# Half of the other two column blocks of a down projection by seven block products, and its operand sums made by accumulating transfers

## The chip, the cores and the metric

The kernel runs on one core of a Trainium2 chip. The metric is device time in microseconds (us), the median of three runs. A profile is one further execution of the same program, recorded by the hardware profiler.

## The reference

Two layers of an encoder on 256 tokens of 2048 numbers in float32. Each layer has an attention part, which this change doesn't touch, and an MLP (multi-layer perceptron) with 8192 inner columns:

```python
    h = rmsnorm(x, norm_mlp[l])
    u = jax.nn.relu(jnp.einsum('bsd,df->bsf', h, w_up[l]))
    x = x + jnp.einsum('bsf,fd->bsd', u * u, w_down[l])
```

The last line is the down projection: 256 x 8192 by 8192 x 2048.

## The kernel before

**Precision.** TensorE (PE) multiplies in a rounded 32-bit format. So each operand is split into a rounded part ("hi") and its remainder ("lo"), and a product of two operands is made of three: hi by hi, lo by hi, hi by lo. Weights arrive from memory in tiles of 128 x 1024 (512 KB). `split` (L1013, L1014) makes the two parts: ScalarE (ACT) casts to `whi`, then VectorE (DVE) subtracts into `wlo`. There are three buffers for each of the two.

**Steps.** The program is a list of steps, one for each weight tile or sum of tiles. The main loop goes through the list. At step i it issues on the SyncE (SP) queue the loads up to step i+6, emits the splits up to step i+2, and emits the preparations (`prep`) up to step i+4 (`LOOK_PREP` = 5), and then the products of step i. What it emits is put by the tile framework into one fixed instruction order for each engine, and each engine works its list strictly in that order.

**Groups.** The 8192 inner columns are worked in 8 groups of 1024. For each group there are 16 up steps (`up_steps`, L673 and L678: eight products of 512 columns and eight of 256, from which ACT and DVE make `uT` and, in `sums_of`, `sT`), and the down steps of the same group of rows of `w_down`, for four blocks of 512 output columns, j = 0 to 3. Up steps of group g+1 are mixed with down steps of group g.

**Plain down steps** (`down_steps`, helper `mode_b`, L466) take one tile of 256 rows of one block j: 12 products of 128 x 512 (two blocks of tokens, two blocks of rows, three parts). In groups 0 to 5 the blocks j = 2 and 3 take four such steps each. Their sum stays in two PSUM banks and is added to the residual `x` by DVE at the end (L723).

**Seven products** (`strassen_steps`, L795). The blocks j = 0 and 1 are worked as a product of 2 x 2 blocks: two blocks of tokens, rows of `w_down` in an even and an odd half, two blocks of columns. Seven products (P1, P2, P7, P6, P5, P3, P4 in this order) take the place of eight, at the price of sums on both sides. The sums of the left side are `sT`. On the right, with B11, B12, B21, B22 the four tiles as stored, P1 uses B11 and P2 uses B21; then B11 gets B12 added (call it B11'), P7 uses B12 + B22, P6 uses t2 = B22 + B11', P5 uses B11', P3 uses B22, and P4 uses t2 + B21. Every product is made for two tiles (h = 0, 1), so there are 14 steps of 6 products of 128 x 512. After the second tile the bank is added to or taken from `x` by DVE (L771). Three banks are in use: "b" from the common pool of six, and "a" and "d", the two halves of the tile `S`, of which there is one.

**The sums on the right** are made in two ways. B11' and t2 + B21 come by an accumulating transfer: a DMA issued on the GpSimd (POOL) queue (`on_top`, L781) that adds the tile from memory to what lies in the buffer. B12 + B22 (L816) and t2 (L822) are additions of 128 x 1024 on DVE.

The tiles B12 and B22 lie in the pool `side` (four buffers, loads at L993), B11 in `spare0` or `spare1` (one buffer each), t2 in the pool `big` (24 buffers).

## Time and profile before

| | |
|---|---|
| median of 3 runs | 2006.74 us (2006.64 to 2006.88) |
| the profiled execution's own time | 2007.62 us |
| its span, first to last instruction | 2005.8 us |
| mean granted TensorE clock | 0.999 |
| PE busy | 1992.2 us, 10206 products |
| DVE, ACT, POOL busy | 1600.0, 1216.0, 337.8 us |
| memory traffic | 420.62 MB, 210 GB/s over the span |
| groups 0 to 5 of the first layer | about 365 to 875 us of the span |

Groups of instructions are named by the line, the engine, the operation and the buffers (output, then inputs); behind the bar stand their busy time, the mean time of one, and the idle time of the engine before them with what ended it. The windows give the busy time of each engine in a stretch. "PEld" is the loading of the left operand into the array, which runs beside the products. In the chain of waits each piece has its start, its length and its line.

### The profile page before, as it was taken

The page shows a single profiled execution, that of the slowest core. Times are in us where ns is not written, and L with a number is a line of the kernel's source. Part 1 is how long each engine was busy: PE and PEld are TensorE (multiplying, and loading weights), DVE is VectorE, ACT ScalarE, POOL GpSimd, SP SyncE. Part 2 cuts the span into 40 slices and gives each one's busy share as a digit, 9 for nine tenths or more (in the row PEclk, how much of TensorE's full clock was granted, in tenths as well). Part 3 has the DMA queues.
Part 4 walks back from the last instruction along what each step waited for, and adds up shares of the span by engine and source line. Part 5 has one row for each costly group of instructions (what it writes and reads, how often), then busy time and mean ns, then how long its engine had stood idle before and what let it go on. Part 6 is the DMA issues. An engine that isn't in the chain of part 4 may idle for free.

```text
span 2005.8 us, 28051 instructions
## 1 busy us (share of the span) xinstructions
PE 1992.2 (99%) x10206; PEld 1698.6 (85%) x10206; DVE 1600.0 (80%) x2121; ACT 1216.0 (61%) x1742; POOL 337.8 (17%) x394
## 2 busy tenths in 40 slices
PE   9999999999999999999999999999999999999998
PEld 7888888888888888888888888888888888888887
DVE  6777877878788888888857688777888888888887
ACT  7657756565655656566657677565655556565664
POOL 0674520000000000000008745100000000000000
PEclk9999999999999999999999999999999999999999
DMA  9755655778787787877766465557787776877774
GB/s 338 215 160 158 210 167 190 218 211 239 210 234 212 218 224 207 246 207 235 207 190 197 147 179 196 179 190 215 208 245 215 232 211 208 243 210 237 198 236 144
DMA packets 118838, 420.62 MB, mean 210 GB/s; under 512 B 13571, under 2 KB 15875, under 8 KB 118700
## 3 DMA queue, kind: packets, MB, share of 16 engines
q1 hardware_dynamic: 109052, 384.18, 59.3%
q0 software_dynamic: 9216, 33.56, 10.2%
q8 instruction: 80, 1.31, 0.3%
q10 hardware_dynamic: 432, 1.10, 0.1%
q14 instruction: 58, 0.48, 0.1%
HBM read 412.99 MB, written 2.11 MB: 207 GB/s over the span
## 4 chain that ended last, share of the span: by engine, by line
PE 95%; DVE 1%; DMA 1%; ACT 1%; issue 1%; SPq 0%; POOL 0%; POOLq 0%; DVEq 0%; ACTq 0%
PE mm L466 40%; PE mm L673 23%; PE S L795 13%; PE mm L678 12%; PE mm L795 2%; PE tr L380 1%; DMA wraw<-in_w_in_dram 1%; PE tr L399 1%; PE S L343 1%; PE S L342 1%; PE tr L223 1%; DVE wlo L1014 0%; ACT big L360 0%; PE tr L392 0%; PE tr L255 0%
## 5 line engine op out<-in xcount | busy, mean ns | idle before, releaser
L1014 DVE TENSOR_TENSOR wlo<-wraw,whi 128x1024 fp32r<-128x1024 f32 (+1 forms) x553 | 680.3, 1232 | 241.5 <-ACT whi L1013 238.7
L1013 ACT CAST whi<-wraw 128x1024 fp32r<-128x1024 f32 (+1 forms) x553 | 579.9, 1051 | 453.8 <-PE mm L466 170.8
L466 PE MATMUL mm<-whi,big 128*128 128x512 f32 (+1 forms) x2172 | 613.2, 386 | 0.6 <-ACT whi L1013 0.6
L673 PE MATMUL mm<-big,whi 128*128 128x512 f32 x2048 | 509.5, 391 | 0.0
L466 PEld LDWEIGHTS mm<-whi,big 128*128 128x128 f32 x2172 | 404.4, 188 | 80.2 <-ACT whi L1013 1.6
L673 PEld LDWEIGHTS mm<-big,whi 128*128 128x128 f32 x2048 | 377.6, 188 | 74.5
L466 PE MATMUL mm<-wlo,big 128*128 128x512 f32 (+1 forms) x1086 | 355.5, 384 | 0.0
L678 PEld LDWEIGHTS mm<-big,wlo 128*128 128x128 f32 x2048 | 279.4, 190 | 20.0
L678 PE MATMUL mm<-big,wlo 128*128 128x256 f32 x2048 | 285.6, 282 | 0.0
L466 PEld LDWEIGHTS mm<-wlo,big 128*128 128x128 f32 x1086 | 204.3, 188 | 38.0
L795 PE MATMUL S<-whi,big 128*128 128x512 f32 x768 | 209.1, 394 | 0.0
L781 POOL DMA_DIRECT2D spare<-in_w_down_dram x32 | 28.0, 876 | 745.8 <-DVE wlo L1014 671.2
L795 PEld LDWEIGHTS S<-whi,big 128*128 128x128 f32 x768 | 134.9, 189 | 21.3 <-DVE x L771 1.0
L466 PE MATMUL mm<-spare,big 128*128 128x512 f32 (+1 forms) x606 | 140.2, 380 | 0.0
L466 PEld LDWEIGHTS mm<-spare,big 128*128 128x128 f32 x606 | 108.9, 188 | 20.4
L795 PE MATMUL S<-wlo,big 128*128 128x512 f32 x384 | 118.8, 391 | 0.0
L781 POOL DMA_DIRECT2D big<-in_w_down_dram x32 | 27.7, 866 | 492.4 <-DVE wlo L1014 485.5
L1013 ACT CAST whi<-big 128x1024 fp32r<-128x1024 f32 x64 | 67.2, 1050 | 70.3 <-PE mm L673 50.4
L1013 ACT CAST whi<-side 128x1024 fp32r<-128x1024 f32 x64 | 67.2, 1051 | 65.4 <-PE mm L673 41.2
L1014 DVE TENSOR_TENSOR wlo<-big,whi 128x1024 fp32r<-128x1024 f32 x64 | 78.3, 1224 | 32.7 <-ACT whi L1013 32.6
L1013 ACT CAST whi<-spare 128x1024 fp32r<-128x1024 f32 x64 | 67.4, 1053 | 52.1 <-PE mm L673 40.8
L1014 DVE TENSOR_TENSOR wlo<-spare,whi 128x1024 fp32r<-128x1024 f32 x64 | 78.0, 1219 | 23.9 <-ACT whi L1013 23.8
(158 smaller groups left out, 2100.3 us busy)
## 6 DMA issues: line engine op xcount, KB each, us to landing
wraw<-in_w_up_dram SPq DMA_DIRECT2D x256, 512.0 KB, 4.4
wraw<-in_w_down_dram SPq DMA_DIRECT2D x160, 512.0 KB, 4.1
wraw<-in_w_in_dram SPq DMA_DIRECT2D x119, 512.0 KB, 3.7
wraw<-in_w_o_dram SPq DMA_DIRECT2D x64, 512.0 KB, 3.7
side<-in_w_down_dram SPq DMA_DIRECT2D x64, 512.0 KB, 4.4
spare<-in_w_down_dram SPq DMA_DIRECT2D x32, 512.0 KB, 4.5
spare<-in_w_down_dram POOLq DMA_DIRECT2D x32, 512.0 KB, 5.8
big<-in_w_down_dram POOLq DMA_DIRECT2D x32, 512.0 KB, 6.5
```

What stands on the lines that cost most here:

```text
L223: nc.tensor.transpose(psv[:, kk, t, :], x[:, t, c0:c0 + P], ident)
L342: nc.tensor.matmul(o, st, u.kh[:, kh, :], start=True, stop=False)
L343: nc.tensor.matmul(o, st, u.kl[:, kh, :], start=False, stop=True)
L380: nc.tensor.transpose(ps[:, c * P:(c + 1) * P], u.p[:, s, kb * P:(kb + 1) * P], ident)
L399: nc.tensor.matmul(ps, u.V[:, kb, u.kv, :, :], pt[:, kb, :], start=n == 0, stop=n == 3)
L466: nc.tensor.matmul(banks[t][:, 0:n], a, (wl if part == "hl" else wh)[:, i, :], start=first and i == 0 and part == "hh", stop=last and i == ...
L673: nc.tensor.matmul(box["b"][fs], wh[:, kk, fs * P:(fs + 1) * P], ht, start=s == 0 and kk == 0, stop=False, skip_group_check=True)
L678: nc.tensor.matmul(box["b"][fs][:, 0:256], wl[:, kk, fs * P:(fs + 1) * P], ht[:, 0:256], start=False, stop=s == 3 and kk == 3, skip_group_ ...
L781: nc.gpsimd.dma_start(tile, src(par, j, h).rearrange("p (k n) -> p k n", k=2), accum_op=ALU.add)
L795: nc.tensor.matmul(o, ops[i][a], w[:, i, :], skip_group_check=True, start=fresh and h == 0 and i == 0 and a == 0 and w is wh, stop=h == 1 ...
L1013: last_act[0] = nc.scalar.copy(h[:, part], w[:, part]).ins
L1014: last_lo[0] = nc.vector.tensor_sub(lo[:, part], w[:, part], f(h[:, part])).ins
```

## The change

In groups 0 to 5 of both layers the blocks j = 2 and 3 are also worked by seven products, for one of the two tiles only (`strassen_steps(g, 1, (0,), 4)`: 7 steps of 6 products). The other half of the rows stays with plain steps: two of 12 products for j = 3 (`down_steps((g,), 3, (2, 3))`), and two for j = 2 at the end of the group, which go on summing into the banks "b" and "d" of the second set of seven products. So the second set isn't evacuated after P2 and P4, and these two plain steps evacuate both.

In all groups B12 + B22 is now made by an accumulating transfer as well, prepared up to seven steps ahead of its use (`LOOK_T3`). Of the sums on the right only t2 is left on DVE. In the first set it is prepared up to six steps ahead (`LOOK_T2` = 7), in the second set up to three (4).

The order of steps within groups 0 to 5 is new: one step of seven products, alternating with an up or plain step, two of the first set being neighbours in two places; then the second set alternating with seven up steps; and at the end the two plain steps of j = 2. The next group begins at once with its first P1. Numbering the 41 steps of a group from 0, the first set stands at 0, 2, 4, 6, 8, 10, 12, 14, 15, 17, 19, 21, 22, 24, the second at 26, 28, ... 38, the plain steps of j = 2 at 39 and 40. Before, a group had 38 steps and began with two plain steps. `w_down` is packed differently on the host, so that each tile is still one contiguous block. The argument `skip_group_check` concerns a check at build time.

```diff
-    LOOK_LOAD, LOOK_SPLIT, LOOK_PREP, BUDGET = 7, 2, 5, 2.2
+    LOOK_LOAD, LOOK_SPLIT, LOOK_PREP, LOOK_T2, LOOK_T3, BUDGET = 7, 2, 5, 7, 8, 2.2
...
-        def down_steps(gs, j):
+        def down_steps(gs, j, ks=range(4), shared=None):
             out_, box = [], {}
-            tiles = [(g, k) for g in gs for k in range(4)]
+            tiles = [(g, k) for g in gs for k in ks]
...
-                        box["b"] = [mm_bank(), mm_bank()]
+                        box["b"] = [shared["b"], shared["d"]] if shared else [mm_bank(), mm_bank()]
...
-                    mode_b(box["b"], hts, wh, wl, [0, 1], n == 0, last, blocks=(0,) if final else (0, 1),
+                    mode_b(box["b"], hts, wh, wl, [0, 1], n == 0 and not shared, last, blocks=(0,) if final else (0, 1),
...
-                out_.append(Step(w_down[l, (g * 4 + j) * 4 + k], 2, 512, None, mm, fourth=gs == (7,)))
+                ti = (g * 4 + j) * 4 + k if g >= 6 else g * 16 + 12 + (j - 2) * 2 + k - 2
+                out_.append(Step(w_down[l, ti], 2, 512, None, mm, fourth=gs == (7,)))
             return out_
-        def strassen_steps(g):
+        def strassen_steps(g, pair=0, tiles=(0, 1), look=LOOK_T2):
...
             raw, t2, box, done = {}, {}, {}, set()
             def src(par, j, h):
-                return w_down[l, g * 16 + (par * 2 + j) * 2 + h]
+                return w_down[l, g * 16 + ((par * 2 + j) * 2 + h if pair == 0 else 8 + par * 2 + j)]
...
+            def sum_of(to, a, b):
+                with tc.issue_after(last_lo[0]):
+                    nc.vector.tensor_add(to, a, b)
             def on_top(tile, par, j, h):
                 nc.gpsimd.dma_start(tile, src(par, j, h).rearrange("p (k n) -> p k n", k=2), accum_op=ALU.add)
             out_ = []
             for name, lf, bk, fresh, dst in plan:
-                for h in range(2):
+                for h in tiles:
                     def mm(wh, wl, name=name, lf=lf, bk=bk, fresh=fresh, dst=dst, h=h):
                         if (name, h) == ("P1", 0):
...
-                                                 stop=h == 1 and i == 1 and w is wl)
-                        if h == 1:
+                                                 stop=h == tiles[-1] and i == 1 and w is wl)
+                        if h == tiles[-1] and not (pair and name in ("P2", "P4")):
                             evac(o, *dst)
                             if g == 7 and name in ("P3", "P4"):
                                 layer_end(l, dst[1])
                     loads, prep, get = [], None, None
                     if name == "P1":
-                        loads = [(("B11", h), src(0, 0, h), lambda h=h: spare(F32, h))]
+                        loads = [(("B11", h), src(0, 0, h), lambda h=h + pair: spare(F32, h))]
                         get = lambda h=h: raw["B11", h]
                     elif name == "P2":
+                        loads = [(("B12", h), src(0, 1, h), None)]
                         def prep(h=h):
                             assert ("P1", h) in done
                             on_top(raw["B11", h], 0, 1, h)
                     elif name == "P7":
-                        loads = [(("B12", h), src(0, 1, h), None), (("B22", h), src(1, 1, h), None)]
                         def prep(h=h):
-                            with tc.issue_after(last_lo[0]):
-                                nc.vector.tensor_add(raw["B12", h], raw["B12", h], raw["B22", h])
+                            on_top(raw["B12", h], 1, 1, h)
                         get = lambda h=h: raw["B12", h]
                     elif name == "P6":
+                        loads = [(("B22", h), src(1, 1, h), None)]
                         def prep(h=h):
                             t2[h] = big(F32, 2, 512)
-                            with tc.issue_after(last_lo[0]):
-                                nc.vector.tensor_add(t2[h], raw["B22", h], raw["B11", h])
+                            sum_of(t2[h], raw["B22", h], raw["B11", h])
                         get = lambda h=h: t2[h]
                     elif name == "P5":
                         def prep(h=h):
...
                         done.add(key)
                         return get()
                     stp = Step(src(1, 0, h) if name == "P2" else None, 2, 512, None, mm, fourth=False, prep=prep,
+                               look={"P6": look, "P7": LOOK_T3}.get(name, LOOK_PREP),
                                raw=operand if get else None,
                                loads=[(raw, k, v, w) for k, v, w in loads])
                     out_.append(stp)
-            return out_
+            return out_, box
         steps.extend(up_steps(0))
         for g in range(8):
             if g < 6:
-                ss = down_steps((g,), 2) + down_steps((g,), 3) + up_steps(g + 1)
+                up = up_steps(g + 1)
+                ss = up[0:4] + down_steps((g,), 3, (2, 3)) + up[4:]
             elif g == 6:
                 ss = up_steps(7)
             else:
                 ss = down_steps((6, 7), 2) + down_steps((6,), 3) + down_steps((7,), 3)
-            hs = strassen_steps(g)
-            order = [0, 0]
-            for p_ in range(7):
-                order += [1, 0, 1]
-                if p_ < 6:
-                    order += [0] * (2 if g < 6 else g == 6) + [0] * (g != 6 and p_ in (1, 3, 5))
-            order += [0] * (len(ss) - order.count(0))
+            hs, _ = strassen_steps(g)
+            if g < 6:
+                more, shared = strassen_steps(g, 1, (0,), 4)
+                hs += more
+            if g < 6:
+                order = []
+                for p_ in range(7):
+                    order += [1, 0, 1] + [0] * (p_ in (0, 1, 2, 4))
+                order += [0, 1] * 7 + [0, 0]
+                ss += down_steps((g,), 2, (2, 3), shared)
+            else:
+                order = [0, 0]
+                for p_ in range(7):
+                    order += [1, 0, 1]
+                    if p_ < 6:
+                        order += [0] * (g == 6) + [0] * (g == 7 and p_ in (1, 3, 5))
+                order += [0] * (len(ss) - order.count(0))
             assert order.count(0) == len(ss) and order.count(1) == len(hs), (order.count(0), order.count(1))
             steps.extend(hs.pop(0) if o else ss.pop(0) for o in order)
...
-        while npr < min(len(steps), i + LOOK_PREP):
-            if steps[npr].prep:
-                steps[npr].prep()
-            npr += 1
+        for k in range(i, min(len(steps), i + 8)):
+            if k < i + steps[k].look and steps[k].prep:
+                steps[k].prep()
+                steps[k].prep = None
...
+    if g < 6:
+        plain[2:4] = [np.stack([b[[par, par + 2], :, j * 512:(j + 1) * 512].transpose(1, 0, 2).reshape(P, 1024)
+                                for par in range(2) for j in (2, 3)]), plain[2][2:4], plain[3][2:4]]
```

Three places show how the order of instructions moves. The first is TensorE at the border of two groups, here groups 4 and 5 of the first layer. `S` is the tile with the banks "a" and "d"; `mm` are other banks. Before:

```order
L466 MATMUL mm_1453_7552<-wlo_1449_7536,big_1396_7253 128x512 [waits DVE_49]
L466 MATMUL mm_1453_7552<-wlo_1449_7536,big_1396_7253 128x512
L466 MATMUL mm_1454_7553<-wlo_1449_7536,big_1396_7253 128x512 x2
L795 MATMUL S_1461_7590<-whi_1451_7548,big_1375_7125 128x512 [waits DVE_49,Activation_49]
L795 MATMUL S_1461_7590<-whi_1451_7548,big_1396_7253 128x512
L795 MATMUL S_1461_7590<-whi_1451_7548,big_1375_7125 128x512
L795 MATMUL S_1461_7590<-whi_1451_7548,big_1396_7253 128x512
L795 MATMUL S_1461_7590<-wlo_1452_7549,big_1375_7125 128x512 [waits DVE_49]
L795 MATMUL S_1461_7590<-wlo_1452_7549,big_1396_7253 128x512
```

And now:

```order
L468 MATMUL mm_1439_7372<-wlo_1478_7579,big_1326_6795 128x512 [waits DVE_49]
L468 MATMUL mm_1439_7372<-wlo_1478_7579,big_1326_6795 128x512
L468 MATMUL S_1433_7338<-wlo_1478_7579,big_1326_6795 128x512 x2
L675 MATMUL mm_1494_7651<-big_632_3155,whi_1484_7610 128x512 [waits Activation_49]
L675 MATMUL mm_1495_7652<-big_632_3155,whi_1484_7610 128x512 [waits PE_49]
L675 MATMUL mm_1494_7651<-big_632_3155,whi_1484_7610 128x512
L675 MATMUL mm_1495_7652<-big_632_3155,whi_1484_7610 128x512
L675 MATMUL mm_1494_7651<-big_634_3165,whi_1484_7610 128x512
L675 MATMUL mm_1495_7652<-big_634_3165,whi_1484_7610 128x512
L675 MATMUL mm_1494_7651<-big_634_3165,whi_1484_7610 128x512
L806 MATMUL S_1490_7637<-whi_1481_7592,big_1368_7010 128x512 [waits DVE_49]
L806 MATMUL S_1490_7637<-whi_1481_7592,big_1410_7236 128x512
```

Before, plain products stand ahead of the first product into the new `S`. Now the plain products themselves write the old `S` (its half "d"), and seven products of the next up step have been put between them and the first product into the new `S`, which waits for DVE. What that wait is for stands on VectorE, at the same border, from the split of the up step's weights on; L728 is the evacuation of a plain step:

```order
L1037 TENSOR_TENSOR wlo_1485_7611<-wraw_1466_7524,whi_1484_7610 128x1024
L696 TENSOR_TENSOR mid_1474_7569<-mid_1472_7559 128x256
L661 TENSOR_TENSOR big_1473_7566<-mid_1472_7559,big_1473_7566 128x512
L697 SCALAR_TENSOR_TENSOR mid_1474_7569<-mid_1474_7569,mid_1472_7559 128x128
L728 TENSOR_TENSOR x_78<-x_78,mm_1439_7372 128x512
L698 SCALAR_TENSOR_TENSOR mid_1474_7569<-mid_1474_7569,mid_1472_7559 128x128
L728 TENSOR_TENSOR x_78<-x_78,S_1433_7338 128x512
L1037 TENSOR_TENSOR wlo_1489_7633<-spare_1469_7537,whi_1488_7632 128x1024
```

The evacuation of the old `S` is the last but one of these rows.

The second place is VectorE inside group 4, from the split of the second set's B11 (`spare_1406`) to its t2 (L788), which reads the same buffer after the accumulating transfer:

```order
L1037 TENSOR_TENSOR wlo_1426_7299<-spare_1406_7207,whi_1425_7298 128x1024
L701 TENSOR_TENSOR big_1412_7243<-mid_1411_7239,big_1412_7243 128x512
L777 TENSOR_TENSOR x_78<-x_78,S_1343_6866 128x512
L1037 TENSOR_TENSOR wlo_1429_7313<-wraw_1413_7246,whi_1428_7312 128x1024
L1037 TENSOR_TENSOR wlo_1432_7335<-wraw_1417_7261,whi_1431_7334 128x1024
L777 TENSOR_TENSOR x_78<-x_78,S_1433_7338 128x512
L1037 TENSOR_TENSOR wlo_1436_7349<-wraw_1420_7273,whi_1435_7348 128x1024
L1037 TENSOR_TENSOR wlo_1438_7369<-side_1416_7259,whi_1437_7368 128x1024
L1037 TENSOR_TENSOR wlo_1442_7382<-wraw_1427_7310,whi_1441_7381 128x1024
L788 TENSOR_TENSOR big_1443_7385<-side_1430_7332,spare_1406_7207 128x1024
```

Between the two stand the splits of the steps 27 to 31, two evacuations (L777) and the end of an up step's work (L701). In the first set more steps lie between: its first B11 is split for step 0, and its t2 stands behind the split of step 8.

The third place is the POOL queue, which holds nothing but accumulating transfers here. Before, two groups:

```order
L781 DMA spare_1294_6705<-in_w_down_dram 128x1024
L781 DMA spare_1300_6739<-in_w_down_dram 128x1024
L781 DMA big_1363_7041<-in_w_down_dram 128x1024
L781 DMA big_1370_7078<-in_w_down_dram 128x1024
L781 DMA spare_1434_7460<-in_w_down_dram 128x1024
L781 DMA spare_1440_7494<-in_w_down_dram 128x1024
L781 DMA big_1503_7796<-in_w_down_dram 128x1024
L781 DMA big_1510_7833<-in_w_down_dram 128x1024
```

And now, a little more than one group (`side` is B12 + B22, `spare` is B11', `big` is t2 + B21):

```order
L792 DMA big_1296_6614<-in_w_down_dram 128x1024
L792 DMA spare_1316_6731<-in_w_down_dram 128x1024
L792 DMA spare_1322_6766<-in_w_down_dram 128x1024
L792 DMA side_1416_7259<-in_w_down_dram 128x1024
L792 DMA big_1363_6972<-in_w_down_dram 128x1024
L792 DMA big_1374_7026<-in_w_down_dram 128x1024
L792 DMA side_1479_7588<-in_w_down_dram 128x1024
L792 DMA side_1486_7628<-in_w_down_dram 128x1024
L792 DMA spare_1406_7207<-in_w_down_dram 128x1024
L792 DMA big_1443_7385<-in_w_down_dram 128x1024
L792 DMA spare_1463_7502<-in_w_down_dram 128x1024
L792 DMA spare_1469_7537<-in_w_down_dram 128x1024
```

Nine transfers stand where four stood, and the transfers of the next group's B12 come ahead of the second set's B11' (`spare_1406`).

13 lines of the change are left out of this document (7 added, 6 removed).

## The prediction

> **What bounds the kernel now.** I read the page's busy times first, then its chain, then what PE waited for.
>
> ```profile
> span 2005.8 us, 28051 instructions
> PE 1992.2 (99%) x10206; PEld 1698.6 (85%) x10206; DVE 1600.0 (80%) x2121; ACT 1216.0 (61%) x1742; POOL 337.8 (17%) x394
> PE 95%; DVE 1%; DMA 1%; ACT 1%; issue 1%; SPq 0%; POOL 0%; POOLq 0%; DVEq 0%; ACTq 0%
> PE tr L255 <- ACT big L515: 2.3, 2, 1.1
> PE mm L1025 <- DVE warm L1020: 1.6, 1, 1.6
> PE tr L255 <- ACT big L565: 1.2, 2, 1.0
> PE mm L466 <- ACT whi L1013: 0.6, 1, 0.6
> ```
>
> TensorE is busy 99% of the span, and its waits sum to 5.7 us, none of them in the down steps. So a product that is no longer made is worth its whole issue time, as long as nothing new makes PE wait. Whether something does is read from the groups that change:
>
> ```profile
> 790.00:875.00 85.00, 85.00 (x436) 72.70 (x435) 69.30 (x85) 48.64 (x59) 3.49 (x4) 1.00 0.76 220
> 875.00:960.00 85.00, 85.00 (x436) 72.70 (x435) 77.41 (x98) 53.30 (x64) 5.24 (x6) 1.00 0.79 233
> 900.00:920.00 20.00, 20.00 (x108) 17.27 (x108) 19.70 (x25) 12.66 (x15) 1.75 (x2) 1.00 0.88 249
> ```
>
> The columns are the stretch, its length, the busy time of PE, PEld, DVE, ACT and POOL, the granted clock, the share of the DMA engines and GB/s. The first row is a stretch of a group's length before the change, the second holds group 6, where seven-product steps alternate with up steps one by one, as they will in groups 0 to 5. There DVE is busy 91%, and in the third row 98.5%, and PE still doesn't miss anything. This row is the strongest evidence that I have.
>
> **What is removed.** The price of a step is read from the chain of waits in order of time (start, length, what), at a place where PE alone is on it:
>
> ```profile
> 453.04 1.36 PE S L795 x6
> 454.40 2.72 PE mm L466 x12
> 474.80 1.81 PE mm L673 x8
> 476.62 0.95 PE mm L678 x8
> 477.57 1.39 PE S L795 x6
> ```
>
> A product of 512 columns takes 2.72/12 = 0.227 us. Per group, the blocks j = 2 and 3 took 8 steps of 12 = 96 products; now they take 7 x 6 + 4 x 12 = 90. Six products in each of 12 groups are 72, at 0.227 us: 16.3 us. (The 0.03 us by which an S step behind an up step is longer are taken back by that up step, 2.76 for 2.79, so they don't count.)
>
> **What is added, and what hides it.** Per group there are three more steps (41 for 38), so three more casts and splits; five more evacuations of 128 x 512 (12 of seven-product banks and 4 plain for 7 and 4); and one DVE sum less (three t2 for two t2 and two B12 + B22). From the groups of the whole run and a stretch of the timeline (start, length):
>
> ```profile
> L1014 DVE TENSOR_TENSOR wlo<-wraw,whi 128x1024 fp32r<-128x1024 f32 x551 | 678.9, 1234 | 241.5 <-ACT whi L1013 238.7 <-ACT mid L651 1.3 <-PE tr L223 0.4
> L1013 ACT CAST whi<-wraw 128x1024 fp32r<-128x1024 f32 x551 | 578.7, 1052 | 453.7 <-PE mm L466 170.8 <-PE mm L673 158.8 <-PE S L795 64.6
> L816 DVE TENSOR_TENSOR side<-side,side 128x1024 f32<-128x1024 f32 x32 | 39.0, 1217 | 0.0
> L652 DVE TENSOR_TENSOR mid<-mid,mm 128x256 f32<-128x256 f32 x128 | 47.6, 413 | 0.0
> ...
> 408.64 0.42 DVE L694 TENSOR_TENSOR mid<-mid 128x256 f32<-128x256 f32 x1
> 408.98 0.69 DVE L659 TENSOR_TENSOR big<-mid,big 128x512 fp32r<-128x512 f32 x1
> 409.58 0.28 DVE L695 SCALAR_TENSOR_TENSOR mid<-mid,mid 128x128 f32<-128x128 f32 x1
> 409.78 0.68 DVE L771 TENSOR_TENSOR x<-x,S 128x512 f32<-128x512 f32 x1
> 410.37 1.12 PE L678 MATMUL mm<-big,wlo 128*128 128x256 f32 x8
> 410.38 0.28 DVE L696 SCALAR_TENSOR_TENSOR mid<-mid,mid 128x128 f32<-128x128 f32 x1
> 410.57 1.05 ACT L1013 CAST whi<-spare 128x1024 fp32r<-128x1024 f32 x1 [0.87 <-PE mm L673]
> 410.58 1.22 DVE L1014 TENSOR_TENSOR wlo<-wraw,whi 128x1024 fp32r<-128x1024 f32 x1
> 411.71 1.22 DVE L1014 TENSOR_TENSOR wlo<-spare,whi 128x1024 fp32r<-128x1024 f32 x1
> ```
>
> Back to back, DVE instructions start closer together than they last: 0.34 us (L694), 0.60 (L659, L771), 0.20 (L695), 1.13 (a split). So DVE gets 3 x 1.13 + 5 x 0.60 - 1.14 = 5.3 us more, 69.3 + 5.3 = 74.6 us in a group of 84.0 us (14 x 1.38 + 8 x 2.72 + 16 x 2.77 = 85.4 before, less 6 x 0.227): 89%, less than the 91% of the second window. ACT gets 3 x 1.05 = 3.2 us on 48.6, POOL five issues on 3.5 us, and SP as many loads as before (16 + 16). These I cost at nothing: PE's own products cover them. Where DVE can't keep up, the price is the whole of the added 5.3 us x 12 = 64 us; the two windows speak against it.
>
> The same stretch shows a delay that I need next: PE goes over to the second pass of an up step at 410.37, and the cast that waits for the first pass starts at 410.57, so a result of PE counts 0.20 us after PE has left it.
>
> **The border of two groups** is the first new wait. Call T the time at which PE leaves step 40, the last plain product. The new `S` can be written when DVE has evacuated the old one, and that is at best 0.20 (PE's result) + 0.60 (evacuation of "b") + 0.20 (L698) + 0.68 (evacuation of "d") = T + 1.68. The seven up products in between last 7 x 0.227 = 1.59 us. So about 0.1 us is lost even if DVE stands ready. It does so narrowly: the split of the up step waits for a cast, which waits for the first pass of step 39 (left at T - 2.72 - 0.91), and so ends at T - 3.63 + 0.20 + 1.05 + 1.13 = T - 1.25; L696, L661 and L697 take it to T - 0.1. With DVE one split late the loss is about 1.2 us. There are five such borders per layer (group 6 begins with two up steps, which cover it). I take 0.25 each: 10 x 0.25 = 2.5 us; ends 1 and 12. Behind the waiting product stand all others of PE, so nothing of it is won back.
>
> **The hand-over from the first set to the second** is alike. `S` is free once P4 (step 24) is evacuated, and the up step 25 covers 2.77 us. From the split of step 23 on, that evacuation included, DVE has four splits, two of the L652 kind (413 ns, 0.37 with the overlap), five of 512 columns (two evacuations and the kinds of L653, L659 and L699) and three small ones: 4 x 1.13 + 2 x 0.37 + 5 x 0.60 + 0.34 + 2 x 0.20 = 9.0 us. It starts when PE has left the first pass of step 20, 7.8 us before the end of step 24, plus 0.20 and a cast of 1.05: 6.5 us before. So it ends 2.5 us after, 0.2 us before PE needs it. I take 0.1 us in each of 12 groups: 1.2 us; ends 0 and 12 (one split late).
>
> **The start of group 0.** Two plain steps used to lie between the last up product of group 0 and the step that reads its last `uT`.
>
> ```profile
> 360.97 1.12 PE L678 MATMUL mm<-big,wlo 128*128 128x256 f32 x8
> 366.53 0.68 DVE L659 TENSOR_TENSOR big<-mid,big 128x512 fp32r<-128x512 f32 x1
> ```
>
> From PE's leaving (360.97 + 0.95) `uT` took until 366.53 + 0.68, 5.3 us. Now steps 0 and 1 cover 4.1 us, and PE's new order puts one product and six of step 3 before the first reader, 1.6 more: 5.7. I take 0.2 us per layer, 0.4; ends 0 and 3 (half a cast and a split late, twice).
>
> **The second set's t2.** DVE now waits in its strict order for the accumulating transfer into B11'. Behind it are all splits, so PE waits soon after.
>
> ```profile
> 367.77 1.22 DVE L1014 TENSOR_TENSOR wlo<-spare,whi 128x1024 fp32r<-128x1024 f32 x1
> 369.30 0.88 POOL L781 DMA_DIRECT2D spare<-in_w_down_dram  x1 [4.44 <-DVE wlo L1014]
> DMA to landing us min/median/max: 5.2/6.3/8.8
> ```
>
> The transfer is issued 0.3 us after the split of B11 (step 26) and lands 5.2 to 8.8 us later: 5.5 to 9.1 us. From that split to t2 stand five splits, each held to PE's pace by its cast: steps 24 to 28, three S and two up, 3 x 1.38 + 2 x 2.77 = 9.7 us. Then t2's cast and split have about 1.6 us to spare before PE needs them. So it fits while a transfer lands within 11 us. I take 0.7 us in all for single late ones; ends 0 and what the second rival gives.
>
> **The sum.** -16.3 + 2.5 + 1.2 + 0.4 + 0.7 = -11.5 us. The profiled execution's own time is 2007.62 us, its span 2005.8 with 1.8 us around it; it would go to 1996.1. The median, 0.9 us lower, goes from 2006.74 to **1995.2 us**.
>
> **Rivals.**
>
> *All new waits are hidden.* DVE runs ahead at the borders, too. Then 2006.74 - 16.3 = 1990.4 us. For it speaks that group 6 loses nothing at 98.5% DVE, and a row of the wait list for the seven-product steps, by which PE's sequencer hardly ever waited for an evacuation of `S` before:
>
> ```profile
>   DVE x L771: 1.0, 3
> ```
>
> Against it: at the border even a ready DVE is 0.1 us late. Chance 0.15.
>
> *The transfers come late, slower than before.* A group moves 41 tiles for 36, nine of them accumulating for four. From the DMA rows of groups 0 to 5 (365 to 875 us: packets, MB, share), and of the first 40 us:
>
> ```profile
> q1 hardware_dynamic: 27419, 99.87, 60.5%
> q0 software_dynamic: 3456, 12.58, 15.2%
> ...
> q1 hardware_dynamic: 4644, 13.39, 90.6%
> ```
>
> A plain tile takes 510 us x 0.605 / 190 tiles = 1.62 us of all 16 engines, an accumulating one 510 x 0.152 / 24 = 3.23. Then 32 plain and 9 accumulating tiles need 81 of 84.0 us, 96%. But the first 40 us show plain tiles at 40 x 0.906 / 25.5 = 1.42 us, so packets get shorter where the queues are full, and it is 75 to 81 us. If landing grows to twice its 6.3 us, t2 is late by 12.6 + 0.3 - 11.3 = 1.6 us in each of 12 groups, 19 us: 1995.2 + 19 = 2014 us. It decides from a landing of 12.0 us on. By the Trainium skill (DMA: Bandwidth & Descriptors, Where 436 GB/s comes from), loads from HBM are bound at about 358 GB/s for a core. By that figure the estimate for 41 tiles of 0.524 MB is 60 us per group, far from a bound, and the sum stays as it is. The last of the three rows, 13.39 MB in 40 us or 335 GB/s, agrees; but the figure doesn't count an accumulating transfer twice, and the row does, so I go by the row. Chance 0.11.
>
> *DVE is half a split late at both hand-overs of `S`.* Then 10 x 0.7 + 12 x 0.4 more than nothing, and with 1 us for t2 and starts 13 us are given back: 2003.4; with a whole split late 10 x 1.2 + 12 x 0.9 + 1 = 24 us, 2014. So around 2006 this is no change. Chance 0.08.
>
> *PE's pauses cost more than their length.* If each border made the rest of its two steps (6 products of S, one and eight of the up step: 1.36 + 1.18 us) run at half pace, 10 x 2.5 = 25 us, 2020 us. The Trainium skill (TensorE: Matmul & The Clock Gate, A second HAM failure mode: psum-queue depth-cycling) tells of short pauses between groups of matmuls, as banks are cycled, that made the clock oscillate. Against it stands this row, where PE pauses for 1.1 us of 20 at a granted clock of 1.00:
>
> ```profile
> 200.00:220.00 20.00, 18.87 (x102) 15.69 (x101) 14.91 (x21) 15.90 (x33) 13.86 (x16) 1.00 0.71 225
> ```
>
> Chance 0.01. *The change doesn't do what it says* (the 72 products aren't saved): the instruction order has them gone, so I give it nothing.
>
> **Chances.** The forecast has 0.65 and the rivals 0.15, 0.11, 0.08 and 0.01. About 0.2%, 4 us, can be told from no change here. Faster by more: the forecast (a few cases of it, 0.02, end within 4 us) and the first rival, 0.78 in all, and a third of the third rival, 0.03: 0.81. Same: 0.02 and 0.05 of the third rival: 0.07. Slower: 0.12. The range goes from all stalls hidden, 1990.0, to 2004.5, which leaves the slow cases and half of the third rival out, some 0.17.
>
> **What would show it.** PE's products fall from 10206 by 72, with PE busy all through 365 to 875 us but for 0.1 to 1 us just before the first `S` product of groups 1 to 5, put down to DVE's L728. Twelve groups that shrink from 85.4 to 84.0 us each plus that pause would show the main term. DVE busy near 75 us per 84 shows the cover; more than 80 would prove it wrong. DMA share of 0.85 or more with POOL landings still under 9 us disproves the second rival; a DVE wait of over 1 us ahead of L788 proves it. The prediction fails if the split or t2 wait on transfers in every group, or if the hand-over at step 26 costs as much as the border.

## The result, and the profile after

The changed kernel takes **1995.51 us** (median of 6 runs, 1995.27 to 1996.13) beside 2006.81 us for the kernel before (6 runs, 2006.64 to 2007.64): a ratio of 0.9942, with a 95% interval of 0.9930 to 0.9955, so 11.3 us faster. The profiled execution took 1995.70 us. Its span and its busy times, from the page of the changed kernel:

```profile
span 1993.9 us, 28351 instructions
PE 1980.3 (99%) x10134; PEld 1683.2 (84%) x10134; DVE 1647.0 (83%) x2197; ACT 1247.4 (63%) x1778; POOL 396.4 (20%) x462
```

72 products are gone, PE's busy time fell by 11.9 us, and so did the span. The groups, by a window of one group's length (same columns as before):

```profile
534.00:618.00 84.00, 84.00 (x429) 71.38 (x428) 73.81 (x92) 51.72 (x61) 7.76 (x9) 1.00 0.87 254
```

DVE has 74 us of work in 84, the DMA share rose from 0.76 to 0.87, and the clock stays at 1.00. PE's own list of waits shows none of the new waits. They stand under the weight loads (PEld). Whether such a wait is felt is read further down, from the length of the step behind it. The columns are us in all, times, and the longest:

```profile
PEld S L806 <- DVE x L777: 2.8, 15, 0.3
PEld S L806 <- DVE x L728: 2.7, 10, 0.4
PEld mm L675 <- ACT whi L1036: 2.2, 12, 0.2
```

L728 evacuates the banks of the plain steps, ten times: the ten borders. Taken by layer, the five of the first wait 1.9 us (up to 0.4), those of the second 0.8 (up to 0.2). One of the first layer in the timeline (start, length, what):

```profile
446.35 1.75 PE L675 MATMUL mm<-big,whi 128*128 128x512 f32 x7
446.51 0.68 DVE L728 TENSOR_TENSOR x<-x,mm 128x512 f32<-128x512 f32 x1
447.11 0.28 DVE L698 SCALAR_TENSOR_TENSOR mid<-mid,mid 128x128 f32<-128x128 f32 x1
447.31 0.68 DVE L728 TENSOR_TENSOR x<-x,S 128x512 f32<-128x512 f32 x1
448.05 0.76 PEld L806 LDWEIGHTS S<-whi,big 128*128 128x128 f32 x4 [0.38 <-DVE x L728]
```

PE has left the last plain product at 446.35. DVE comes to "b" 0.16 us later, straight from the up work ahead of it, does a small piece of up work, and evacuates "d" by 447.99. The first weight load of the new `S` starts at 448.05, 1.70 us after PE left. The same place in the second layer:

```profile
1436.69 0.68 DVE L728 TENSOR_TENSOR x<-x,mm 128x512 f32<-128x512 f32 x1
1436.74 1.75 PE L675 MATMUL mm<-big,whi 128*128 128x512 f32 x7
1437.49 0.68 DVE L728 TENSOR_TENSOR x<-x,S 128x512 f32<-128x512 f32 x1
1438.22 0.77 PEld L806 LDWEIGHTS S<-whi,big 128*128 128x128 f32 x4 [0.15 <-DVE x L728]
```

Here "b" is evacuated from 0.05 us before PE leaves the last plain product, since that product and the one before it write "d" alone; "d" is free 1.43 us after, and the weight load comes 1.48 us after. In the chain of waits the first border, the hand-over inside the next group, two more borders of the first layer, and two of the second look like this:

```profile
448.09 1.61 PE S L806 x6
...
499.29 1.51 PE S L806 x6
...
532.75 1.63 PE S L806 x6
...
617.37 1.61 PE S L806 x6
...
1438.50 1.38 PE S L806 x6
...
1522.89 1.40 PE S L806 x6
```

An S step takes 1.39 us, so a border of the first layer costs 0.22 to 0.24, in all five of them, and one of the second next to nothing (1.36 to 1.40). The hand-over costs 0.10 to 0.13 in both layers. From border to border a group takes 84.62 to 84.66 us in the first layer and 84.36 to 84.42 in the second.

The difference comes from the split ahead of the border (L1037), behind which everything on DVE stands. In the first layer it starts 0.25 us after its cast has ended (444.23, the cast at 442.92 + 1.06), in the second 0.02 after (1434.40, the cast at 1433.32 + 1.06), the same at all five borders of each. What holds it in the first layer these traces don't show.

The transfers, from the DMA rows of groups 0 to 5 (365 to 869 us; packets, MB, share of the engines) and the groups of issues (the last number is the median us to landing; no transfer of POOL's queue took more than 8.8):

```profile
q1 hardware_dynamic: 27600, 100.54, 54.4%
q0 software_dynamic: 7632, 27.79, 32.1%
...
side<-in_w_down_dram POOLq DMA_DIRECT2D x18, 512.0 KB, 7.4
big<-in_w_down_dram POOLq DMA_DIRECT2D x18, 512.0 KB, 6.0
```

504 x 0.544 / 191.8 tiles = 1.43 us for a plain tile, 504 x 0.321 / 53 = 3.05 for an accumulating one. DVE was never idle ahead of t2 (L788).

### The profile page after: what moved, and what is told of

Read it like the earlier page. It is cut to its first block, busy times and chain, and to the rows that moved or that the text cites. A ratio compares the mean times of both kernels' runs of the same rounds, so it can differ in the third digit from the quotient of the medians.

```text
span 1993.9 us, 28351 instructions
## 1 busy us (share of the span) xinstructions
PE 1980.3 (99%) x10134; PEld 1683.2 (84%) x10134; DVE 1647.0 (83%) x2197; ACT 1247.4 (63%) x1778; POOL 396.4 (20%) x462
## 4 chain that ended last, share of the span: by engine, by line
PE 96%; DVE 1%; DMA 1%; ACT 1%; issue 1%; SPq 0%; POOL 0%; POOLq 0%; DVEq 0%; ACTq 0%
PE mm L468 32%; PE mm L675 23%; PE S L806 18%; PE mm L680 12%; PE mm L806 3%; PE S L468 2%; PE tr L380 1%; PE tr L399 1%; DMA wraw<-in_w_in_dram 1%; PE S L343 1%; PE S L342 1%; PE tr L223 1%; DVE wlo L1037 0%; ACT big L360 0%; PE tr L392 0%
## 5 line engine op out<-in xcount | busy, mean ns | idle before, releaser
L1037 DVE TENSOR_TENSOR wlo<-wraw,whi 128x1024 fp32r<-128x1024 f32 (+1 forms) x517 | 634.3, 1233 | 200.9 <-ACT whi L1036 191.4
L675 PE MATMUL mm<-big,whi 128*128 128x512 f32 x2048 | 514.1, 390 | 0.0
L468 PE MATMUL mm<-whi,big 128*128 128x512 f32 (+1 forms) x1692 | 500.1, 384 | 0.8 <-ACT whi L1036 0.8
L675 PEld LDWEIGHTS mm<-big,whi 128*128 128x128 f32 x2048 | 380.5, 188 | 79.4 <-ACT whi L1036 2.2
L468 PEld LDWEIGHTS mm<-whi,big 128*128 128x128 f32 x1692 | 314.3, 188 | 61.8 <-ACT whi L1036 1.9
L680 PEld LDWEIGHTS mm<-big,wlo 128*128 128x128 f32 x2048 | 280.9, 190 | 21.2
L468 PE MATMUL mm<-wlo,big 128*128 128x512 f32 (+1 forms) x846 | 293.3, 382 | 0.0
L806 PE MATMUL S<-whi,big 128*128 128x512 f32 x1056 | 290.1, 396 | 0.0
L680 PE MATMUL mm<-big,wlo 128*128 128x256 f32 x2048 | 287.3, 282 | 0.0
L806 PEld LDWEIGHTS S<-whi,big 128*128 128x128 f32 x1056 | 184.3, 189 | 34.2 <-DVE x L777 2.8
L468 PEld LDWEIGHTS mm<-wlo,big 128*128 128x128 f32 x846 | 159.3, 188 | 28.7
L806 PE MATMUL S<-wlo,big 128*128 128x512 f32 x528 | 163.4, 391 | 0.0
L1036 ACT CAST whi<-side 128x1024 fp32r<-128x1024 f32 x88 | 92.5, 1051 | 85.3 <-PE mm L675 76.6
L1037 DVE TENSOR_TENSOR wlo<-side,whi 128x1024 fp32r<-128x1024 f32 x88 | 107.7, 1224 | 35.4 <-ACT whi L1036 34.6
L1037 DVE TENSOR_TENSOR wlo<-big,whi 128x1024 fp32r<-128x1024 f32 x88 | 107.7, 1224 | 21.5 <-ACT whi L1036 21.3
L806 PEld LDWEIGHTS S<-wlo,big 128*128 128x128 f32 x528 | 99.2, 188 | 22.2
```

The lines of the kernel that those rows point to most:

```text
L468: nc.tensor.matmul(banks[t][:, 0:n], a, (wl if part == "hl" else wh)[:, i, :], start=first and i == 0 and part == "hh", stop=last and i == ...
L675: nc.tensor.matmul(box["b"][fs], wh[:, kk, fs * P:(fs + 1) * P], ht, start=s == 0 and kk == 0, stop=False, skip_group_check=True)
L680: nc.tensor.matmul(box["b"][fs][:, 0:256], wl[:, kk, fs * P:(fs + 1) * P], ht[:, 0:256], start=False, stop=s == 3 and kk == 3, skip_group_ ...
L806: nc.tensor.matmul(o, ops[i][a], w[:, i, :], skip_group_check=True, start=fresh and h == 0 and i == 0 and a == 0 and w is wh, stop=h == ti ...
L1036: last_act[0] = nc.scalar.copy(h[:, part], w[:, part]).ins
L1037: last_lo[0] = nc.vector.tensor_sub(lo[:, part], w[:, part], f(h[:, part])).ins
```

## The experiments

A ratio is that to the kernel before, run on the same chip beside it, with its 95% interval.

### The border: a whole up step ahead of each group

```diff
-                order = []
+                order = [0]
...
-                    order += [1, 0, 1] + [0] * (p_ in (0, 1, 2, 4))
+                    order += [1, 0, 1] + [0] * (p_ in (0, 1, 2))
```

> The changed kernel, but groups 0 to 5 begin with an up step, which is taken from behind the ninth S step. So a whole up step (2.77 us) lies between the last plain step of a group and the first S step of the next, where seven up products (1.59 us) lay. Theory (the new S waits for DVE's evacuation of the old S): the loss of 0.22 to 0.24 us at each of ten borders goes, 1995.5 - 2.3 = 1993.2 us, and the wait list has no S step that waits for the evacuation at L728. Rival (the longer first S step is a matter of the neighbours of the weight loads, not of DVE): it stays at 1995.5, and the first S step still takes 1.6 us.

Measured: 2001.04 us (7 runs), ratio 0.9971 (0.9959 to 0.9982). The border of the first layer is as the theory has it (in the second there was hardly anything to win), and the time went the other way: 5.5 us slower than the changed kernel. From the chain of waits, around one border and later in the same group:

```profile
534.09 1.39 PE S L806 x6
...
553.17 1.15 DVE wlo L1037
...
554.53 0.59 DVE x L728
555.12 0.20 DVE mid L698
555.33 0.60 DVE x L728
555.92 1.15 DVE big L788
...
558.11 1.05 ACT whi L1036
...
559.20 1.89 PE mm L675 x7
```

The first S step of the group is back to 1.39 us. But with the up step moved, the end of the plain j = 3 sum (two L728) comes right ahead of t2 (L788) in DVE's order, t2 is late, ACT's cast of t2 waits for it, and the cast for the next up step stands behind that one. So PE waits 0.35 us there, which it didn't before, and weight loads of S steps wait 39 times for an evacuation at L777 where they waited 15 times. From border to border it is 84.98 (534.09 to 619.07): 0.23 us won and 0.6 lost in each group of the first layer. In the second, where a group takes 85.02 to 85.04 us, 0.6 are lost and nothing is won.

### Two S tiles

```diff
-        return pp.tile([P, 512], F32, tag="bank", bufs=6, name=nm("mm"))
+        return pp.tile([P, 512], F32, tag="bank", bufs=4, name=nm("mm"))
...
-        return pp.tile([P, 4, 256], F32, tag="S", bufs=1, name=nm("S"))
+        return pp.tile([P, 4, 256], F32, tag="S", bufs=2, name=nm("S"))
```

> The changed kernel with two S tiles in PSUM for one, and four banks for six in the other pool. Theory: an S step never waits for an evacuation of the S before it, so the borders (10 x 0.23) and the hand-overs inside the groups (12 x 0.11) are won back: 1995.5 - 3.6 = 1991.9 us. Rival: with four banks the other chains of products wait for a free bank, in attention above all, and it is slower than 1995.5 although the S waits are gone; then the wait list shows PE waiting at a line other than that of the S products.

Measured: 2010.55 us (11 runs), ratio 1.0013 (1.0004 to 1.0022). Both held, each at its place. The chain shows borders without the longer piece, 84.24 us apart:

```profile
624.27 1.36 PE S L806 x6
...
708.51 1.36 PE S L806 x6
```

84.62 - 84.24 = 0.38 us per group are won in the first layer, a little more than border and hand-over (0.34). In the second, where a group takes 84.23 to 84.31 us, it is about 0.12, the hand-over alone. That makes 6 x 0.38 + 6 x 0.12 = 3.0 us, and they are lost six times over elsewhere, which I followed only in part: in 40 to 200 us of the span PE is busy 156.57 of 160 us, where the changed kernel has 160.00, and attention's transposes (L380, 18 waits, 6.9 us) head the list of its weight loads. So the price of the hand-overs of `S` is shown, and saving it this way costs more than it brings.

### The set without the transfers, the transfers without the set

First B12 + B22 back on DVE, with the new set kept:

```diff
-                            on_top(raw["B12", h], 1, 1, h)
+                            sum_of(raw["B12", h], raw["B12", h], raw["B22", h])
```

> The changed kernel, but B12 + B22 are summed on DVE as before the change, in all groups and in the new set of seven products too (three more sums of 1.22 us per group, three accumulating transfers fewer). Theory (the products saved make the gain, and DVE has room): DVE goes from 74.4 to 77.8 us in a group of 84.6, 92%, and the time stays within 2 us of 1995.5. Rival (the accumulating transfers are what makes room for the extra set): splits fall behind at the hand-overs of S and in the stretches with two S steps in a row, half a split (0.6 us) or more in each of 12 groups at two places, 14 us or more, so 2009 or slower.

Then the steps, products and packing of before, with B12 + B22 by transfers:

> The kernel before with one part of the change: B12 + B22 by an accumulating transfer, seven or eight steps ahead; the steps, the products and the packing of the weights are those before. Theory (DVE's time is not what bounds): DVE loses 32 sums, 39 us of busy time in all, and the time stays at 2006.8 within 1.5 us. Rival (DVE is on the path in the groups): 2 to 5 us faster than before. Third: transfers that land late make it slower, with DVE waiting for a DMA ahead of a split.

Measured: 2000.81 us (5 runs), ratio 0.9967 (0.9955 to 0.9980), for the set alone; 2007.88 us (11 runs), ratio 1.0004 (0.9995 to 1.0012), for the transfers alone. So the set alone is worth 6.0 us, the transfers alone nothing that can be measured, though they take 32.6 us off DVE's busy time (1600.0 to 1567.4), and both together 11.3. The transfers pay only beside the set, by 5.3 us: more than my theory's 2, less than the rival's 14. The wait list of the set alone shows what they pay for:

```profile
PEld S L806 <- DVE wlo L1037: 5.1, 12, 0.5
PEld mm L675 <- ACT whi L1036: 4.1, 12, 0.3
```

Once per group an S step waits for a split, though DVE is busy no more than 76.6 of 84 us. In group 1 of the first layer it is the split at 477.13. From 460.11 up to it DVE works without a gap, and one of the sums put back (461.25) stands near the start of that stretch; in the changed kernel DVE still has gaps there, the longest 0.45 us (ahead of 467.66). From the first S step of group 0 to that of group 6, the groups of the first layer take 2.0 us more than in the changed kernel, and those of the second, where no border wait goes in return, 3.0. That is nearly the whole of the 5.3. A full group without a longer border takes 84.79 us in the first layer (533.83 to 618.62) and 84.76 to 84.78 in the second; each group 0 loses 1.0.

### Three and six more transfers, unbound

```diff
+                            if g < 6:
+                                on_top(scratch, 1, 1, h)
```

> The changed kernel with three more accumulating transfers of 0.52 MB in each of groups 0 to 5, issued right behind those of B12 + B22, onto a scratch tile that nothing reads; one buffer fewer (23 for 24) in the pool named big makes room for it. By the changed kernel's own rows (1.43 us of all DMA engines for a plain tile, 3.05 for an accumulating one) the DMA engines need 32 x 1.43 + 12 x 3.05 = 82.4 us of a group's 84.6. Theory (the engines have room until their time is full): within 2 us of 1995.5. Rival (landing grows well before they are full): the second set's t2 comes late, DVE waits ahead of L788 and 5 us or more are lost.

> As the kernel with three more, but six more per group: three behind those of B12 + B22 and three behind those onto t2, all onto the same scratch tile. By the same rows the DMA engines need 32 x 1.43 + 15 x 3.05 = 91.5 us of 84.6. Theory (the price of 3.05 us holds): the groups become as long as the transfers, 12 x 6.9 = 83 us more, about 2078, with the DMA share near 1. Rival (packets get shorter as the queues fill, or the two waits of an accumulating packet overlap): the share stays under 1, and it is less than 20 us slower.

Measured: 2120.43 and 2231.5 us (ratios 1.0559, 1.0543 to 1.0575, and 1.1124, 1.1105 to 1.1144). They answer another question than mine. The scratch tile waits for nothing in the program, so the transfers were issued at once. The row of that line with three more (count, ns min/median/max, first and last start):

```profile
L794 POOL DMA_DIRECT2D scratch<-in_w_down_dram x36: 839/872/1137, 2.4 to 252.6; - x36
```

All of them stood one behind the other on POOL's queue in the first 253 us (514 with six more), each waiting for the one before, and POOL's work for attention stood behind them. Nothing on landing follows from the two.

### Seven products for all tiles, with sums on POOL or by transfers

Groups 0 to 5 without any plain down step; first B12 + B22 on POOL:

```diff
-                    order += [1, 0, 1] + [0] * (p_ in (0, 1, 2, 4))
-                order += [0, 1] * 7 + [0, 0]
+                order = ([0] + [1, 0, 1] * 7) * 2
...
-                            on_top(raw["B12", h], 1, 1, h)
+                            nc.gpsimd.tensor_add(raw["B12", h], raw["B12", h], raw["B22", h])
```

> A further step: groups 0 to 5 compute the blocks j = 2 and 3 with seven products for all of their tiles (14 more S steps of six products for 7 and 4 plain steps of twelve), each half of a group begins with an up step, and B12 + B22 are summed on POOL in all groups. Six products fewer per group again, 12 x 6 x 0.227 = 16.3 us, and the borders' 2.3 us go. Theory: DVE has three more splits and one more t2 per group, 74.4 + 3 x 1.13 + 1.14 = 78.9 us of 83.0, 95%, which is less than the 98.5% that group 6 bore without a wait: 1995.5 - 16.3 - 2.3 = 1977 us, up to 1983 with small waits. Rival: at 95% DVE runs late at both hand-overs of S, 12 x 2 x 0.6 = 14 us given back, about 1991 or slower; or the sums on POOL, some 2.7 us each by its adds of 128 x 512 in 1.35 us, delay the transfers that POOL issues behind them.

Then the same order of steps with B12 + B22 by transfers:

> As the further step, but B12 + B22 by accumulating transfers, as in the changed kernel: 12 accumulating and 32 plain tiles in a group, 82.4 us of DMA time by the changed kernel's rows in groups of 83.0 us. Theory (room until the time is full): as fast as the kernel with the sums on POOL, within 2 us. Rival (landing grows near the full time): t2 comes late, and it is 5 us or more slower than that one, with DVE waiting for a DMA ahead of L788.

Measured: 2049.06 us (ratio 1.0207, 1.0192 to 1.0222) on POOL, 1987.62 us (4 runs, 1983.76 to 1992.08; ratio 0.9896, 0.9880 to 0.9913) by transfers. With POOL the theory is off by some 70 us; it isn't the queue that costs, and the rival named the wrong thing. In the timeline of the kernel with sums on POOL:

```profile
446.17 2.40 POOL L826 TENSOR_TENSOR side<-side,side 128x1024 f32<-128x1024 f32 x1 [14.39 <-DVE wlo L1031]
447.27 2.38 DVE L1031 TENSOR_TENSOR wlo<-wraw,whi 128x1024 fp32r<-128x1024 f32 x1 [1.24 <-ACT whi L1030]
449.58 1.21 DVE L1031 TENSOR_TENSOR wlo<-spare,whi 128x1024 fp32r<-128x1024 f32 x1
```

A split of DVE lasts 1.21 us, and 2.38 where it meets a sum on POOL. DVE's busy time is 1762.8 us against 1680.3 with as many instructions (2221), 82 us more, and PE waits for splits. The Trainium skill (SBUF — State Buffer, Who interferes with whom) says that a DVE instruction with both inputs in SBUF contends with a GpSimd instruction that reads SBUF. The two rows agree.

The kernel with all sums by transfers is faster than the changed one, but 10 us behind 1977. Its profile is of an execution of 1992.08 us. Undisturbed, its half group takes 41.64 us (500.61 to 542.25 in its chain); the three most disturbed ones of the first layer take 44.20, 43.46 and 43.80 (583.85 to 715.31). POOL's queue and ACT at such a place:

```profile
589.23 0.86 POOL L792 DMA_DIRECT2D side<-in_w_down_dram  x1 [13.21 <-DMA side<-in_w_down_dram]
589.76 1.22 POOL L792 DMA_DIRECT2D big<-in_w_down_dram  x1
592.21 0.86 POOL L792 DMA_DIRECT2D side<-in_w_down_dram  x1 [1.23 <-DMA side<-in_w_down_dram]
592.76 1.20 POOL L792 DMA_DIRECT2D big<-in_w_down_dram  x1
...
610.78 1.04 ACT L1032 CAST whi<-big 128x1024 fp32r<-128x1024 f32 x1 [5.66 <-DMA big<-in_w_down_dram]
```

The transfers onto t2 (`big`) stand behind those of the next set's B12 + B22 (`side`), which wait for a load; four go out within 3.5 us, and the last lands 17.9 us later. A cast waits 5.66 us for it.

### Three more transfers, held to their place

```diff
+                            if g < 6:
+                                nc.scalar.copy(scratch[h][:, 0, 0:1], raw["B12", h][:, 0, 0:1])
                             on_top(raw["B12", h], 1, 1, h)
+                            if g < 6:
+                                on_top(scratch[h], 1, 1, h)
```

> The changed kernel with three more accumulating transfers per group, now held to their place: each goes onto one of two scratch tiles into which ACT first copies a column of the loaded B12, so that it can't be issued before the transfer of B12 + B22 next to it (two buffers fewer, 22 for 24, in the pool named big; nothing reads the scratch tiles). The steps of PE, DVE and, but for that column, ACT are those of the changed kernel; only the transfers per group grow from 41 to 44 tiles, as in the kernel with seven products for all blocks: 32 x 1.43 + 12 x 3.05 = 82.4 us of 84.6. Theory (the transfers that land 13 us after issue there, and the cast that waits for them, come from the full queues): the transfer of B21 onto t2 lands after 12 us or more here too, the cast waits for it, and it is 6 to 15 us slower than 1995.5. Rival (they come from the other order of steps there, with DVE at 92%): landings stay under 9 us, and it is within 2 us of 1995.5.

Measured: 2056.42 us (4 runs), ratio 1.0239 (1.0225 to 1.0253): 61 us slower than the changed kernel, 5.1 per group. From its chain, in one group:

```profile
598.63 11.98 DMA spare<-in_w_down_dram
```

and from its list of waits on DVE in the groups of the first layer:

```profile
DVE big L791 <- DMA spare<-in_w_down_dram: 17.8, 5, 4.3
```

`spare` is B11' of the second set, L791 is t2 here, which starts at 610.63, when the transfer has landed. Landing of such transfers rose to between 11 and 13 us in five groups of that layer, each time behind four accumulating ones that were issued within 4 us (589.54 to 592.62 here), and DVE waited ahead of t2 for up to 4.3 us. The DMA share of these groups was 0.90. So it was not the transfer that I had expected to be late (that of B21), but the place of the prediction's second rival, late transfers ahead of t2. A part of the 61 us belongs to the scratch column on ACT, which waits for the load of B12 (21.3 us in 14 times in that layer), so the whole isn't the price of three transfers.

### Half of the sums on DVE, by tile and by half of a group

```diff
-                            on_top(raw["B12", h], 1, 1, h)
+                            if h == 1:
+                                sum_of(raw["B12", h], raw["B12", h], raw["B22", h])
+                            else:
+                                on_top(raw["B12", h], 1, 1, h)
```

> Seven products for all tiles of all blocks in groups 0 to 5, with B12 + B22 by a transfer for the first tile of each pair and by DVE for the second: 10 accumulating and 32 plain tiles, 76.3 us of 83.0 (92%), and DVE at 76.6 + 2 x 1.14 = 78.9 us (95%). Theory (the transfers at 95% and more cost the kernel with all sums by transfers some 10 us): most of that comes back, 1977 to 1983 us. Rival (DVE is the nearer bound: three sums per group on DVE cost the changed kernel 5 us): what the transfers give back DVE takes, 1986 us or slower, with S steps that wait for the split or for an evacuation.

> As the kernel mixed by tile, but mixed by half: the first set of each group has both sums by transfers, the second both on DVE. The sums over a group are the same. If what counts is the share over a group, the two are alike within 2 us. If the queues fill and empty within half a group, this one is 3 us slower or more, and the transfers onto t2 land late in the first halves alone.

Measured: 1998.12 us (5 runs), ratio 0.9950 (0.9938 to 0.9962), by tile; 2002.2 us (8 runs), ratio 0.9972 (0.9962 to 0.9983), by half. The rival is right: what the transfers give back DVE takes, and more. The split by half is 4 us slower. Its own expectation had the late transfers in the first halves, and the trace has them in the second. From POOL's queue and from ACT, in the first layer:

```profile
429.43 1.22 POOL L792 DMA_DIRECT2D big<-in_w_down_dram  x1
443.16 1.05 ACT L1038 CAST whi<-big 128x1024 fp32r<-128x1024 f32 x1 [2.68 <-DMA big<-in_w_down_dram]
```

This transfer onto t2 (`big`) belongs to a second set, and stands behind the sums by transfer of the next group's first set. ACT waits so once per group, five times in all and 11.8 us: the same order of POOL's queue as in the kernel with all sums by transfers. That this is the whole of the 4 us isn't shown.

### All by transfers, with POOL's queue in order

```diff
-                            on_top(raw["B12", h], 1, 1, h)
+                            with tc.issue_after(last_t4[0]) if last_t4[0] is not None else nullcontext():
+                                on_top(raw["B12", h], 1, 1, h)
...
-                            on_top(t2[h], 1, 0, h)
+                            last_t4[0] = on_top(t2[h], 1, 0, h)
```

> The kernel with seven products for all tiles and all sums by transfers, with one constraint on POOL's queue: the transfers of B12 + B22 of the next set are issued behind those of B21 onto t2 of the set before. In the run without it POOL issued side, big, side, big within 3.5 us, after a wait of 13.2 us for the load of B12, and the two big ones landed 13 and 18 us after their issue, with a cast that waited for them. Four accumulating tiles at 3.05 us are 12.2 us of the engines. Theory (the burst and its order are what makes them late, not the share over a group, which stays at 95%): the transfers onto t2 land within 9 us, casts wait for them no more, and 1987.6 goes to 1980 to 1984 us; what stays of the loss are S steps that wait for an evacuation. Rival (at 95% the queues are full whatever the order): landings of 12 us or more, only at another place, and 1986 to 1990 us.

Measured: **1980.35 us** (4 runs, 1979.95 to 1980.54), ratio 0.9864 (0.9847 to 0.9880). This is 26.7 us faster than the kernel before it and 15 us faster than the change. The queue, and a window of groups 0 to 5:

```profile
588.34 0.86 POOL L792 DMA_DIRECT2D big<-in_w_down_dram  x1 [13.04 <-DVE wlo L1034]
592.62 0.87 POOL L792 DMA_DIRECT2D big<-in_w_down_dram  x1 [3.41 <-DVE wlo L1034]
593.16 2.11 POOL L792 DMA_DIRECT2D side<-in_w_down_dram  x2
```

```profile
365.00:869.00 504.00, 504.00 (x2568) 426.47 (x2568) 468.53 (x571) 332.94 (x389) 63.06 (x73) 1.00 0.97 277
```

The transfers onto t2 go out as soon as their split is done and land after 7.9 us in the median (13.4 before). Those of B12 + B22 now take 13.0, and nothing waits for them. Every half group takes 41.6 us, at a DMA share of 0.97. The rival was right that landings of 12 us or more turn up at another place; that a share of 95% is itself the bound is disproved.

The same window of the kernel mixed by tile, which is 18 us slower:

```profile
365.00:869.00 504.00, 500.96 (x2524) 419.60 (x2523) 470.54 (x572) 326.71 (x380) 51.32 (x59) 1.00 0.91 261
```

A half group there is 42.4 us long, 0.76 us more, though DVE is idle for 7% of the time: 79.2 us of work in a group, which would be 95% of the ordered kernel's 83.3. What counts is where the sum stands. One half group of the kernel mixed by tile:

```profile
581.26 1.22 DVE L788 TENSOR_TENSOR side<-side,side 128x1024 f32<-128x1024 f32 x1
600.49 1.22 DVE L1039 TENSOR_TENSOR wlo<-wraw,whi 128x1024 fp32r<-128x1024 f32 x1
601.76 1.01 PEld L680 LDWEIGHTS mm<-big,wlo 128*128 128x128 f32 x8 [0.69 <-DVE wlo L1039]
```

From the sum at 581.26 to the split that PE needs (600.49) DVE has but one gap, of 0.23 us: 20.27 us of work in 20.50. So it can't make up for the sum before that split is due. Weight loads of L680 wait 12 times for a split in the window above, once per half group, 7.9 us in all. DVE's idle time lies elsewhere in the half group. This kernel's queue isn't put in order, which could be a second cause; but no cast waits for a transfer onto t2 in that window, and the chain ahead of this wait runs from 587.20 on over DVE and ACT, not over a transfer.

## Why the prediction was right, and where it wasn't

**The sum** was -11.5 us, the runs show -11.3, and the span -11.9. The main term stands: 72 products are gone and the step prices are the same. That the number is so close is in part luck: two of the losses that I forecast were some 2 us too large, and they are made up by one that I had at nothing.

**The border** was the term I had worked out most closely, and it is the one that the runs correct most. I took 2.5 us; ten borders cost about 1.2, all of it in the first layer. The failed step is the best case, `S` free at T + 1.68. It has the evacuation of "b" wait until T for PE, but the last two plain products write "d" alone, as the instruction order shows, and in the second layer "b" is evacuated from T - 0.05 and "d" free at T + 1.43. A DVE that comes in time hides the border. In the first layer `S` is free at T + 1.64, near my figure, but for another reason: the instruction behind the split starts at T - 0.97 and not at T - 1.25, so DVE comes to "b" at T + 0.16 where I had T - 0.1. That the wait is one for the evacuation is shown twice: it goes with a whole up step in between, and with a second `S`. Taken by my own sign of failing, the hand-over as dear as the border, the account of the border fails in the second layer.

**The hand-over** at step 26 was taken at 0.1 us, and it is 0.10 to 0.13 in all twelve groups. It and the first layer's borders disprove the first rival, by which all new waits were hidden; for the second layer's borders that rival is right.

**t2 and the start of group 0.** Taken at 0.7 and 0.4 us. t2 never made DVE wait. At the start of group 0 two S steps waited for the last `uT`, 0.9 us in all of the weight loads' waits in the two layers, of which 0.1 to 0.2 us per layer is felt.

**The loss that I had at nothing.** A group shrank from 85.49 us (453.04 to 538.53 before) to 84.62 in the first layer, by 0.87 and not by 1.36. Border and hand-over explain 0.34 of the difference of 0.49. In the second layer it is 84.39, and the hand-over explains 0.11 of 0.26. In both 0.15 us are left, 1.8 us in twelve groups. They are spread over small pieces of the chain, where the products of two steps are put into another order than I assumed: an S step of 1.41 to 1.45 us between three and five products of an up step's second pass, and that up step's first pass of 1.85 for 1.81, ahead of which a weight load waits up to 0.2 us for a cast (the row of L675 above, once per group).

**DVE** was forecast at 74.6 us of 84 and has 73.8 to 74.1 in full groups. But the argument that I rested on it is wrong as a rule. I held 89% against stretches that had borne 91 and 98.5%, and took the lower share as cover. The sums put back on DVE cost the changed kernel 5.3 us at 91%, and the kernel mixed by tile loses 18 us to the ordered one with DVE idle for 7% of the time. What fails is to read cover from a busy share: the share of a group doesn't say whether DVE has a gap between the added work and the next split that PE needs. In both kernels it has next to none there.

**The second rival**, late transfers, didn't come about at 41 tiles per group: they take 32 x 1.43 + 9 x 3.05 = 73.2 us of 84.6, where I had 75 to 81 of 84. But the kernel stood closer to it than my chance of 0.11 says. I had it decide from a landing of 12.0 us; at 11 to 13 us (three more tiles) DVE did wait ahead of t2, up to 4.3 us where I had 1.6 at twice the landing. And the cause isn't the share of the DMA engines, by which I had weighed it: at 0.97 nothing waits for a transfer when the queue is in order, at 0.95 some 7 us are lost when it isn't, and at 0.90 DVE did wait. In these runs landing grew behind accumulating transfers that were issued in a burst. An estimate fits: four of them at 3.05 us are 12.2 us of the engines.

**PE's pauses** (the fourth rival) changed no clock: 1.00 in the windows of the changed kernel's groups. By the Trainium skill (TensorE: Matmul & The Clock Gate, A second HAM failure mode: psum-queue depth-cycling) short pauses can make it oscillate; five waits of 0.4 us and five of 0.15 don't show it here.

## What to carry to other kernels

Ask of each added instruction not what share of its engine it takes but whether the engine has a gap between it and the next instruction that another one waits for: taking B12 + B22 off DVE was worth nothing in the old order of steps, and leaving half of it there cost 0.8 us per half group in the fullest new one, with DVE still idle for 7%. Where several transfers share one queue, look at its order first: the one with the nearest deadline must not stand behind one that waits for a load. And when a step is moved to save a known wait, look at what the step was hiding where it stood.

## What I hadn't expected of the hardware

An accumulating transfer of 512 KB takes 3.05 us of the DMA engines and a plain one 1.43, 2.1 times as much, at a DMA share of 0.87. In the ordered kernel, at a share of 0.97 with 277 GB/s moved, they are 3.00 and 1.40; before the change, at 0.76, they were 3.23 and 1.62.

A DVE subtraction of 128 x 1024 with both inputs in SBUF lasts 2.38 us and not 1.21 while POOL adds two buffers.

The short waits here leave the clock alone, and long ones don't. In the kernel with six more transfers, where PE waited for up to 31 us at a time, two windows in a row show it at 0.78 and 0.81; the first:

```profile
366.00:450.00 84.00, 48.24 (x198) 37.95 (x197) 37.89 (x59) 29.35 (x62) 33.97 (x43) 0.78 0.77 188
```
